# A mixture of softmaxes on one core: rows regrouped so that each partition holds 32 adjacent ones, weights on GpSimd, first batch loaded by head

## The chip, the cores and the metric

The kernel runs on one core of one Trainium2 chip. The metric is the device time in microseconds of that core. Before the change nine runs gave a median of 784.88 us (784.59 to 785.77).

## The reference

For each of 32 x 128 rows there are four heads of 4096 logits and four prior logits. The output row is the sum over the heads of the softmax of the head's logits, weighted by the softmax of the row's prior.

```python
batch, seq, vocab = 32, 128, 4096      # num_heads = 4, all float32
prior_probs = exp(prior - prior.max(-1));  prior_probs /= prior_probs.sum(-1)
softmax = exp(logits - logits.max(-1));    softmax /= softmax.sum(-1)
mixture = np.sum(prior_probs[..., None] * softmax, axis=2)
```

The logits are 268 MB, the output 67 MB, the prior 64 KB. Both kernels leave out the subtraction of the logits' maximum.

## The kernel before

One step of the outer loop (L85) handles one batch: 128 rows, one per partition, each with its four heads, so one tile `ltile` of 128 x 4 x 4096 (64 KB per partition, 8 MB). The sequence position is the partition, so the 128 rows of a tile are adjacent in memory, 64 KB apart, and the tile is one contiguous piece of 8 MB. The stored tile (128 x 4096, 2 MB) is contiguous too.

Loading: `load` (L41 to L46) is issued on SP's queue, as one transfer for batches 0 to 28 and as four transfers of one head each for the last three (`pieces`, L36). There are two `ltile` buffers, so the load of batch b+2 (L121) is issued when ACT has read all heads of batch b. Loads 0 and 1 are issued at the start (L53, L58).

The prior (L56 to L80) is loaded on ACT's queue with the batch on the partition (32 x 512), normalized on DVE and ACT, and turned into `pp` (sequence position on the partition) by 16 transposes of 32 x 32 blocks (L78).

Work on a head h: ACT takes the exponential of the head into `etile` (two buffers) and the row's sum into `dsum` (L100). DVE takes the reciprocal `rden` of the sum (L103), multiplies it by the prior's weight into `coeff` (L104), and then for head 0 writes `acc = etile * coeff` (L106, one tensor input), for heads 1 to 3 `acc = etile * coeff + acc` (L108, two tensor inputs). The small statistics come from a rotating pool of eight buffers. In the last two batches the exponential and the accumulation go into `ltile` itself (`inplace`).

Storing: batch b-1 is stored on ACT's queue during batch b (L90), for b below 29. Batches 28, 29, 30 and 31 are stored on SP's queue (L119 to L126), the last in two halves after each second of four chunks of the last accumulation (L112 to L119). There are two `acc` buffers, so L106 of batch b waits for the store of batch b-2.

The order on each engine is fixed when the kernel is built, by a scheduler that follows the program's order and its own estimates. In the kernel before, ACT has the first exponential of a batch ahead of the store of the batch before it from batch 3 on, and the store ahead in batches 1 and 2.

Of the kernel before, what the change touches and what calls it, by code (L numbers as in the profile page):

```python
# [1 line left out]

# [4 lines left out]

FP32 = mybir.dt.float32
AF = mybir.ActivationFunctionType
ALU = mybir.AluOpType  # L10
AX = mybir.AxisListType


@with_exitstack
def kernel(
    ctx: ExitStack,
    tc: tile.TileContext,
    logits: bass.AP,
    prior: bass.AP,
    out: bass.AP,  # L20
):
    nc = tc.nc
    B, S, H, V = logits.shape
    assert prior.shape == (B, S, H)
    assert out.shape == (B, S, V)
    P = 128
    assert S == P and B == 32

    lpool = ctx.enter_context(tc.tile_pool(name="lpool", bufs=2))
    epool = ctx.enter_context(tc.tile_pool(name="epool", bufs=2))  # L30
    apool = ctx.enter_context(tc.tile_pool(name="apool", bufs=2))
    spool = ctx.enter_context(tc.tile_pool(name="spool", bufs=8))
    cpool = ctx.enter_context(tc.tile_pool(name="cpool", bufs=1))


    def pieces(b):  # L36
        return 1 if b >= B - 3 else H

    ltiles = {}

    def load(b):  # L41
        lt = lpool.tile([P, H, V], FP32, name="ltile")
        n = pieces(b)
        for h in range(0, H, n):
            nc.sync.dma_start(out=lt[:, h : h + n], in_=logits[b, :, h : h + n, :])  # L45
        ltiles[b] = lt  # L46

    accs = {}

    def store(b, lo=0, hi=V, eng=nc.sync):  # L50
        eng.dma_start(out=out[b, :, lo:hi], in_=accs[b][:, lo:hi])  # L51

    load(0)  # L53


    pr = cpool.tile([B, S, H], FP32, name="pr")  # L56
    nc.scalar.dma_start(out=pr, in_=prior)
    load(1)  # L58
    pmax = cpool.tile([B, S], FP32, name="pmax")
    nc.vector.reduce_max(pmax, pr, axis=AX.X)  # L60
    pc = cpool.tile([B, S, H], FP32, name="pc")
    nc.vector.tensor_sub(pc, pr, pmax.unsqueeze(2).to_broadcast([B, S, H]))  # L62
    pe = cpool.tile([B, S, H], FP32, name="pe")
    nc.scalar.activation(pe, pc, AF.Exp)  # L64
    psum = cpool.tile([B, S], FP32, name="psum")
    nc.vector.reduce_sum(psum, pe, axis=AX.X)  # L66
    prec = cpool.tile([B, S], FP32, name="prec")
    nc.vector.reciprocal(prec, psum)  # L68

    pn = cpool.tile([B, H, S], FP32, name="pn")  # L70
    nc.vector.tensor_mul(  # L71
        pn.rearrange("b h s -> b s h"), pe, prec.unsqueeze(2).to_broadcast([B, S, H])
    )

    pp = cpool.tile([P, H, B], FP32, name="pp")
    for t in range(S // 32):
        for h in range(H):
            nc.vector.transpose(  # L78
                pp[32 * t : 32 * (t + 1), h, :], pn[:, h, 32 * t : 32 * (t + 1)]
            )  # L80

    NCHUNK = 4
    CW = V // NCHUNK

    for b in range(B):  # L85
        last = b == B - 1
        inplace = b >= B - 2
        lt = ltiles.pop(b)
        if 0 < b < B - 3:
            store(b - 1, eng=nc.scalar)  # L90
        if not inplace:
            accs[b] = apool.tile([P, V], FP32, name="acc")
        else:
            accs[b] = lt[:, 0]
        acc = accs[b]
        for h in range(H):
            split = last and h == H - 1
            et = lt[:, h] if inplace else epool.tile([P, V], FP32, name="etile")
            dsum = spool.tile([P, 1], FP32, name="dsum")
            nc.scalar.activation(et, lt[:, h], AF.Exp, accum_out=dsum)  # L100
            coeff = spool.tile([P, 1], FP32, name="coeff")
            rden = spool.tile([P, 1], FP32, name="rden")
            nc.vector.reciprocal(rden, dsum)  # L103
            nc.vector.tensor_mul(coeff, rden, pp[:, h, b : b + 1])  # L104
            if h == 0:
                nc.vector.tensor_scalar_mul(out=acc, in0=et, scalar1=coeff)  # L106
            elif not split:
                nc.vector.scalar_tensor_tensor(  # L108
                    out=acc, in0=et, scalar=coeff, in1=acc, op0=ALU.mult, op1=ALU.add
                )  # L110
            else:
                for c in range(NCHUNK):  # L112
                    cs = slice(c * CW, (c + 1) * CW)
                    nc.vector.scalar_tensor_tensor(  # L114
                        out=acc[:, cs], in0=et[:, cs], scalar=coeff, in1=acc[:, cs],
                        op0=ALU.mult, op1=ALU.add,
                    )
                    if c % 2:
                        store(b, (c - 1) * CW, (c + 1) * CW)  # L119
        if b + 2 < B:  # L120
            load(b + 2)  # L121
        if b == B - 3:
            store(b - 1)
            store(b)
        elif b == B - 2:
            store(b)  # L126


# [1 line left out]
_INS = ['logits', 'prior']  # L130
_OUTS = [((32, 128, 4096), 'float32')]


# [23 lines left out]
```

The softmax here doesn't subtract the row's maximum and nothing guards it: scores larger than these inputs give would overflow.

## Time and profile before

| what | value |
|---|---|
| median of 9 runs | 784.88 us |
| profiled execution, device time | 784.97 us |
| its span, first to last instruction | 783.2 us |
| DVE busy | 544.8 us, 408 instructions |
| ACT busy | 472.7 us, 258 instructions |
| POOL busy | 0.2 us, 4 instructions |
| exponential of a head (L100) | 3612 ns |
| first head's multiply (L106) | 2353 ns |
| multiply and add (L108) | 4484 ns |
| reciprocal, weight (L103, L104), one column | 158 and 159 ns |
| transfers: 8 MB load, 2 MB store on ACT's queue, issue to landing | 31.3 and 30.0 us |

DVE is the vector engine, ACT the scalar engine, POOL GpSimd, SP the engine whose queue issues the loads. The DMA line of the slices is the mean busy share of the core's 16 DMA engines, in tenths. Queue q1 is SP's, q10 is ACT's. A transfer of 128 rows is cut into packets of one row each: 64 KB for a whole row of logits, 16 KB for one head or one output row. The windows list gives busy time in us and, last, the DMA share and the bytes moved per time. A line of the waits gives who waited for whom, and then the total in us, the number of times and the longest.

### The profile page before, as it was taken

Reading aid. Unit: us, or ns where it says so; the run is one execution under the profiler, and the core shown is the slowest. Engines: PE = TensorE matmul, PEld = TensorE weight load, DVE = VectorE, ACT = ScalarE, POOL = GpSimd, SP = SyncE. Lnnn points to the kernel's source line nnn. Section 1 sums busy time; section 2 is a strip of 40 time slices with the busy share of each in tenths; the row PEclk is TensorE's granted clock in tenths of the full one; section 3 lists DMA queues with packets and bytes.
Section 4 is the critical chain, followed back from the end, with each engine's and each line's share of the span. In section 5 each row is a group of like instructions: output and inputs, shape, how many; then the busy total and the mean of one; then the engine's idle time right before and its main releaser. Section 6 shows DMA issues by size and latency. Waiting matters only on the chain.

```text
span 783.2 us, 977 instructions
## 1 busy us (share of the span) xinstructions
DVE 544.8 (70%) x408; ACT 472.7 (60%) x258; POOL 0.2 (0%) x4
## 2 busy tenths in 40 slices
DVE  3577688666786667866668766687656876669994
ACT  0766556755557555575555765556755567558971
POOL 0000000000000000000000000000000000000000
DMA  9999999999999999999999999999999999999997
GB/s 378 455 395 459 409 449 421 445 422 442 442 414 443 440 430 438 438 423 438 426 445 420 449 412 455 414 448 421 445 420 447 432 428 433 443 411 431 430 428 325
DMA packets 10712, 335.68 MB, mean 429 GB/s; under 512 B 1200, under 2 KB 1200, under 8 KB 1232
## 3 DMA queue, kind: packets, MB, share of 16 engines
q1 hardware_dynamic: 6624, 276.83, 81.9%
q10 hardware_dynamic: 4080, 58.79, 17.5%
q14 instruction: 8, 0.07, 0.0%
HBM read 268.50 MB, written 67.11 MB: 429 GB/s over the span
## 4 chain that ended last, share of the span: by engine, by line
DMA 76%; DVE 14%; ACT 6%; issue 1%; DVEq 0%; SPq 0%; ACTq 0%
DMA ltile<-in_logits_dram 42%; DMA out_dram<-acc 34%; DVE acc L108 9%; ACT etile L100 6%; DVE acc L106 3%; DVE ltile L108 1%; DVE ltile L114 0%; DVE coeff L104 0%; DVE rden L103 0%; DVE ltile L106 0%; DVEq L152 0%; SPq L45 0%; ACTq L100 0%; ACTq L51 0%; DVEq L106 0%
## 5 line engine op out<-in xcount | busy, mean ns | idle before, releaser
L100 ACT ACTIVATE etile<-ltile 128x4096 f32<-128x4096 f32 x120 | 433.4, 3612 | 277.3 <-DMA ltile<-in_logits_dram 199.2
L108 DVE SCALAR_TENSOR_TENSOR acc<-etile,coeff,acc 128x4096 f32<-128x4096 f32 x90 | 403.6, 4484 | 3.2
L103 DVE RECIPROCAL rden<-dsum 128x1 f32<-128x1 f32 x128 | 20.2, 158 | 157.8 <-ACT etile L100 157.8
L106 DVE TENSOR_SCALAR acc<-etile,coeff 128x4096 f32<-128x4096 f32 x30 | 70.6, 2353 | 49.6 <-DMA out_dram<-acc 49.4
L100 ACT ACTIVATE ltile<-ltile 128x4096 f32<-128x4096 f32 x8 | 28.9, 3611 | 4.8 <-DVE rden L103 2.4
L104 DVE TENSOR_TENSOR coeff<-rden,pp 128x1 f32<-128x1 f32 x128 | 20.3, 159 | 4.4
L108 DVE SCALAR_TENSOR_TENSOR ltile<-ltile,coeff 128x4096 f32<-128x4096 f32 x5 | 22.4, 4484 | 0.2
L100 ACT ACTIVATION_READ_ACCUMULATOR etile<-ltile 128x1 f32 x120 | 22.3, 186 | 0.0
L60 DVE TENSOR_REDUCE pmax<-pr 32x128 f32<-32x512 f32 x1 | 0.7, 674 | 10.9 <-DMA pr<-in_prior_dram 10.9
L64 ACT ACTIVATE pe<-pc 32x512 f32<-32x512 f32 x1 | 0.6, 628 | 9.9 <-DVE pc L62 9.9
L114 DVE SCALAR_TENSOR_TENSOR ltile<-ltile,coeff 128x1024 f32<-128x1024 f32 x4 | 4.9, 1278 | 0.0
L106 DVE TENSOR_SCALAR ltile<-ltile,coeff 128x4096 f32<-128x4096 f32 x2 | 4.7, 2354 | 0.1
L64 ACT ACT_TABLE_LOAD x1 | 1.3, 1283 | 1.2 <-PEq L141 1.2
L78 DVE STREAM_TRANSPOSE pp<-pn 32x32 f32<-32x32 f32 x16 | 1.9, 170 | 0.1
L100 ACT ACTIVATION_READ_ACCUMULATOR ltile<-ltile 128x1 f32 x8 | 1.5, 187 | 0.0
L66 DVE TENSOR_REDUCE psum<-pe 32x128 f32<-32x512 f32 x1 | 0.7, 674 | 0.7 <-ACT pe L64 0.7
L71 DVE TENSOR_TENSOR pn<-pe,prec 32x512 f32<-32x512 f32 x1 | 1.0, 1021 | 0.0
L68 DVE RECIPROCAL prec<-psum 32x128 f32<-32x128 f32 x1 | 0.9, 941 | 0.0
L62 DVE TENSOR_TENSOR pc<-pr,pmax 32x512 f32<-32x512 f32 x1 | 0.7, 678 | 0.0
L141 POOL MEMSET const-uint8-127<- 128x1 uint8 x1 | 0.1, 102 | 0.0
L141 POOL MEMSET const-bfloat16-1.0<- 128x1 bf16 x1 | 0.1, 101 | 0.0
L141 POOL MEMSET const-float32-0.0<- 128x1 f32 x1 | 0.1, 98 | 0.2 <-issue 0.2
(1 smaller groups left out, 0.1 us busy)
## 6 DMA issues: line engine op xcount, KB each, us to landing
out_dram<-acc ACTq DMA_DIRECT2D x28, 2048.0 KB, 30.0
ltile<-in_logits_dram SPq DMA_DIRECT2D x12, 2048.0 KB, 22.9
out_dram<-acc SPq DMA_DIRECT2D x2, 2048.0 KB, 34.1
out_dram<-ltile SPq DMA_DIRECT2D x1, 2048.0 KB, 22.8
out_dram<-ltile SPq DMA_DIRECT2D x2, 1024.0 KB, 10.2
ltile<-in_logits_dram SPq DMA_DIRECT2D x29, 31.3
pr<-in_prior_dram ACTq DMA_DIRECT2D x1, 64.0 KB, 10.2
```

The source lines that it names most:

```text
L60: nc.vector.reduce_max(pmax, pr, axis=AX.X)
L62: nc.vector.tensor_sub(pc, pr, pmax.unsqueeze(2).to_broadcast([B, S, H]))
L64: nc.scalar.activation(pe, pc, AF.Exp)
L68: nc.vector.reciprocal(prec, psum)
L71: nc.vector.tensor_mul(pn.rearrange("b h s -> b s h"), pe, prec.unsqueeze(2).to_broadcast([B, S, H]))
L78: nc.vector.transpose(pp[32 * t : 32 * (t + 1), h, :], pn[:, h, 32 * t : 32 * (t + 1)])
L100: nc.scalar.activation(et, lt[:, h], AF.Exp, accum_out=dsum)
L103: nc.vector.reciprocal(rden, dsum)
L104: nc.vector.tensor_mul(coeff, rden, pp[:, h, b : b + 1])
L106: nc.vector.tensor_scalar_mul(out=acc, in0=et, scalar1=coeff)
L108: nc.vector.scalar_tensor_tensor(out=acc, in0=et, scalar=coeff, in1=acc, op0=ALU.mult, op1=ALU.add)
L114: nc.vector.scalar_tensor_tensor(out=acc[:, cs], in0=et[:, cs], scalar=coeff, in1=acc[:, cs], op0=ALU.mult, op1=ALU.add,)
```

## The change

The rows are numbered 0 to 4095 (batch times sequence). In the new kernel partition p holds rows 32p to 32p+31, and step u of the outer loop handles row 32p+u of every partition. A tile therefore consists of 128 rows that lie 32 rows apart: 2 MiB from partition to partition in the logits, 512 KiB in the output. The prior is loaded with the same row assignment (128 x 32 x 4, 512 bytes per partition), is normalized in place and needs no transposes.

The other edits: step 0 is loaded by head, as the last three are. The statistics `dsum`, `rden` and `coeff` are one column each per head and step in fixed tiles of 128 columns. The two exponential buffers become one fixed tile `ebuf`, and the wait of an exponential for the exponential two before it is declared unneeded. Head 0 is multiplied by the reciprocal and by the weight in one DVE instruction with two scalars. For heads 1 to 3 GpSimd multiplies the weight, 96 instructions in all. The last accumulation is in two chunks rather than four, each stored at once. The first exponential of a step is kept in program order, so that on ACT it follows the store of the step before. On DVE the reciprocal of a head stands directly ahead of the large instruction of the same head.

```diff
+    U = B * S // P
+    lg = logits.rearrange("b s h v -> (b s) h v").rearrange("(p u) h v -> u p h v", u=U)
+    ov = out.rearrange("b s v -> (b s) v").rearrange("(p u) v -> u p v", u=U)
+    pv = prior.rearrange("b s h -> (b s) h").rearrange("(p u) h -> p u h", u=U)
...
     def pieces(b):
-        return 1 if b >= B - 3 else H
+        return 1 if b == 0 or b >= U - 3 else H
...
-            nc.sync.dma_start(out=lt[:, h : h + n], in_=logits[b, :, h : h + n, :])
+            eng.dma_start(out=lt[:, h : h + n], in_=lg[b, :, h : h + n, :])
...
-        eng.dma_start(out=out[b, :, lo:hi], in_=accs[b][:, lo:hi])
+        eng.dma_start(out=ov[b, :, lo:hi], in_=accs[b][:, lo:hi])
...
+    pr = cpool.tile([P, U, H], FP32, name="pr")
+    nc.scalar.dma_start(out=pr, in_=pv)
...
-    for t in range(S // 32):
-        for h in range(H):
-            nc.vector.transpose(
-                pp[32 * t : 32 * (t + 1), h, :], pn[:, h, 32 * t : 32 * (t + 1)]
-            )
...
-    NCHUNK = 4
+    NCHUNK = 2
...
+    dsum = cpool.tile([P, U * H], FP32, name="dsum")
+    rden = cpool.tile([P, U * H], FP32, name="rden")
+    coeff = cpool.tile([P, U * H], FP32, name="coeff")
+    ebuf = cpool.tile([P, 2, V], FP32, name="ebuf")
...
-            nc.scalar.activation(et, lt[:, h], AF.Exp, accum_out=dsum)
...
-            nc.vector.tensor_mul(coeff, rden, pp[:, h, b : b + 1])
+            i = b * H + h
+            col = slice(i, i + 1)
+            et = lt[:, h] if inplace else ebuf[:, h % 2]
+            ex = nc.scalar.activation(et, lt[:, h], AF.Exp, accum_out=dsum[:, col])
             if h == 0:
-                nc.vector.tensor_scalar_mul(out=acc, in0=et, scalar1=coeff)
+                tc.keep_in_program_order(ex)
+            if not inplace:
+                if len(exps) >= 2:
+                    tc.declare_no_dep(ex.ins, exps[-2], reason="covered by the sum")
+                exps.append(ex.ins)
+            nc.vector.reciprocal(rden[:, col], dsum[:, col])
+            if h == 0:
+                nc.vector.tensor_scalar(
+                    out=acc, in0=et, scalar1=rden[:, col], scalar2=pp[:, b, h : h + 1],
+                    op0=ALU.mult, op1=ALU.mult,
+                )
+                continue
+            nc.gpsimd.tensor_mul(coeff[:, col], rden[:, col], pp[:, b, h : h + 1])
```

More of the change, by code (lines that the diff above doesn't have):

```diff
@@ L27, with load @@
     assert S == P and B == 32
+    U = B * S // P
+    lg = logits.rearrange("b s h v -> (b s) h v").rearrange("(p u) h v -> u p h v", u=U)
+    ov = out.rearrange("b s v -> (b s) v").rearrange("(p u) v -> u p v", u=U)
+    pv = prior.rearrange("b s h -> (b s) h").rearrange("(p u) h -> p u h", u=U)
     lpool = ctx.enter_context(tc.tile_pool(name="lpool", bufs=2))
-    epool = ctx.enter_context(tc.tile_pool(name="epool", bufs=2))
     apool = ctx.enter_context(tc.tile_pool(name="apool", bufs=2))
-    spool = ctx.enter_context(tc.tile_pool(name="spool", bufs=8))
     cpool = ctx.enter_context(tc.tile_pool(name="cpool", bufs=1))
     def pieces(b):
-        return 1 if b >= B - 3 else H
+        return 1 if b == 0 or b >= U - 3 else H
     ltiles = {}
-    def load(b):
+    def load(b, eng=nc.sync):
         lt = lpool.tile([P, H, V], FP32, name="ltile")
@@ L50, in store @@
     def store(b, lo=0, hi=V, eng=nc.sync):
-        eng.dma_start(out=out[b, :, lo:hi], in_=accs[b][:, lo:hi])
[L53 to L59, printed above, removed]
-    nc.vector.reduce_max(pmax, pr, axis=AX.X)
[L61 to L72, printed above, removed]
-    )
-    pp = cpool.tile([P, H, B], FP32, name="pp")
-    for t in range(S // 32):
-        for h in range(H):
-            nc.vector.transpose(
-                pp[32 * t : 32 * (t + 1), h, :], pn[:, h, 32 * t : 32 * (t + 1)]
-            )
-    NCHUNK = 4
[L83 to L87, printed above, removed]
+        eng.dma_start(out=ov[b, :, lo:hi], in_=accs[b][:, lo:hi])
+    load(0, eng=nc.sync)
+    pr = cpool.tile([P, U, H], FP32, name="pr")
+    nc.scalar.dma_start(out=pr, in_=pv)
+    load(1, eng=nc.sync)
+    pmax = cpool.tile([P, U], FP32, name="pmax")
+    nc.vector.reduce_max(pmax, pr, axis=AX.X)
+    nc.vector.tensor_sub(pr, pr, pmax.unsqueeze(2).to_broadcast([P, U, H]))
+    nc.scalar.activation(pr, pr, AF.Exp)
+    nc.vector.reduce_sum(pmax, pr, axis=AX.X)
+    nc.vector.reciprocal(pmax, pmax)
+    pp = cpool.tile([P, U, H], FP32, name="pp")
+    nc.vector.tensor_mul(pp, pr, pmax.unsqueeze(2).to_broadcast([P, U, H]))
+    NCHUNK = 2
[3 more added lines that the diff above has]
+    ebuf = cpool.tile([P, 2, V], FP32, name="ebuf")
+    exps = []
+    for b in range(U):
+        last = b == U - 1
+        inplace = b >= U - 2
         lt = ltiles.pop(b)
-        if 0 < b < B - 3:
-            store(b - 1, eng=nc.scalar)
         if not inplace:
@@ L95 @@
         acc = accs[b]
+        if 0 < b < U - 3:
+            store(b - 1, eng=nc.scalar)
         for h in range(H):
             split = last and h == H - 1
[L98 to L103, printed above, removed]
@@ L104 @@
-            nc.vector.tensor_mul(coeff, rden, pp[:, h, b : b + 1])
-            if h == 0:
-                nc.vector.tensor_scalar_mul(out=acc, in0=et, scalar1=coeff)
-            elif not split:
+            i = b * H + h
+            col = slice(i, i + 1)
+            et = lt[:, h] if inplace else ebuf[:, h % 2]
+            ex = nc.scalar.activation(et, lt[:, h], AF.Exp, accum_out=dsum[:, col])
+            if h == 0:
+                tc.keep_in_program_order(ex)
[3 more added lines that the diff above has]
+                exps.append(ex.ins)
@@ new lines @@
+            nc.vector.reciprocal(rden[:, col], dsum[:, col])
[6 more added lines that the diff above has]
+            nc.gpsimd.tensor_mul(coeff[:, col], rden[:, col], pp[:, b, h : h + 1])
+            n = NCHUNK if split else 1
+            w = V // n
+            for c in range(n):
+                cs = slice(c * w, (c + 1) * w)
@@ L108 @@
                 nc.vector.scalar_tensor_tensor(
-                    out=acc, in0=et, scalar=coeff, in1=acc, op0=ALU.mult, op1=ALU.add
-                )
[L111 to L119, printed above, removed]
@@ L120 @@
-        if b + 2 < B:
+                    out=acc[:, cs], in0=et[:, cs], scalar=coeff[:, col], in1=acc[:, cs],
+                    op0=ALU.mult, op1=ALU.add,
+                )
+                if split:
+                    store(b, c * w, (c + 1) * w)
+        if b + 2 < U:
             load(b + 2)
-        if b == B - 3:
+        if b == U - 3:
             store(b - 1)
             store(b)
-        elif b == B - 2:
+        elif b == U - 2:
             store(b)
```

## The prediction

> **What bounds the kernel now.** I read the page's engine and slice parts first, then its queues, then the windows at both ends, then the waits and the timeline of the last batches.
>
> ```profile
> DVE 544.8 (70%) x408; ACT 472.7 (60%) x258; POOL 0.2 (0%) x4
> ...
> DMA  9999999999999999999999999999999999999997
> ...
> q1 hardware_dynamic: 6624, 276.83, 81.9%
> q10 hardware_dynamic: 4080, 58.79, 17.5%
> ...
> HBM read 268.50 MB, written 67.11 MB: 429 GB/s over the span
> ```
>
> No compute engine is full, but the 16 DMA engines are full in all slices but the last. In the queue lines the last column is the share of 16 engines over the span: q1 (SP) takes 81.9% of 783.2 = 641.4 us, q10 (ACT) 17.5% = 137.1 us, together 778.5 us. What is left, 4.7 us, is all the time in which the transfers do not fill the engines. q1 carries the loads (268.44 MB) and five late stores (8.39 MB); at 641.4/276.83 = 2.317 us per MB the loads cost 622.0 us. All stores, 67.11 MB at about 2.32, cost 155.9 us. A whole load row (64 KB, one packet) holds its engine for 64 KB/(434 GB/s/16) = about 2.42 us, a 16 KB row 0.61 us.
>
> ```profile
> 0.00:20.00 20.00, 5.91 (x21) 1.91 (x2) 0.20 (x4) 1.00 1.00 416
> ...
> 40.00:45.00 5.00, 4.72 (x4) 0.00 (x0) 0.00 (x0) 1.00 0.99 393
> 45.00:50.00 5.00, 0.90 (x3) 4.71 (x3) 0.00 (x0) 1.00 0.83 321
> ...
> 160.00:400.00 240.00, 165.61 (x118) 147.27 (x80) 0.00 (x0) 1.00 1.00 432
> ...
> 765.00:770.00 5.00, 4.93 (x6) 0.81 (x2) 0.00 (x0) 1.00 1.00 429
> 770.00:775.00 5.00, 1.92 (x2) 0.00 (x0) 0.00 (x0) 1.00 0.97 413
> 775.00:784.00 9.00, 0.00 (x0) 0.00 (x0) 0.00 (x0) 1.00 0.41 172
> ```
>
> Columns: window, length, DVE, ACT and POOL busy, clock, DMA share, GB/s. There is one hole near 45 us (0.83) and the drain after 775 us (172 GB/s x 9 us = 1.55 MB, 3.6 us of work, so some 5 us of landing and closing). In the middle there is no hole.
>
> ```profile
> ACT etile L100 <- DMA ltile<-in_logits_dram: 199.2, 27, 10.0
> DVE rden L103 <- ACT etile L100: 157.8, 33, 9.0
> ACT etile L100 <- DVE rden L103: 60.7, 54, 1.5
> DVE acc L106 <- DMA out_dram<-acc: 49.4, 26, 2.3
> ```
>
> These waits confirm it: ACT waits for loads 27 times, DVE then waits for ACT. A batch needs 2.35 + 3 x 4.48 + 4 x 0.35 = 17.2 us of DVE against (622.0 + 155.9)/32 = 24.3 us of DMA, so DVE has 7 us of cover per batch. The cover is absent at the end only: in the timeline DVE works without a pause from 719 to 772 us.
>
> **What the Trainium skill says.** (1) "DMA: Bandwidth & Descriptors", Latency and other measured facts: copies of tiles of 128 partitions x 16 KiB between HBM tensors reach 214 GB/s per direction at full rate, 207 with a row pitch of 512 KiB, 164 with 2 MiB, 103 with 4 or 8 MiB; that channels alias is called an inference there. The trace of before has no such pitch: its partitions are 64 KB apart in the loads and 16 KB apart in the stores, and it moves 429 GB/s in both directions together, which agrees with 2 x 214 as the full rate. (2) The same page, Where 436 GB/s comes from: 435 GB/s is the ceiling of the ports. The trace's 432 in mid-run agrees, so no layout can make transfers appreciably faster. (3) "VectorE: DVE Perf Modes", The perf-mode tier table: fp32 tensor_scalar from SBUF runs at two elements per cycle (1227 ns for 2048). L106 with 2353 ns for 4096 agrees. (4) "GPSIMD Engine Reference", 3.1: a two-input elementwise op costs about 2.6 cycles per element after dispatch, 4497 ns for 2048. No run here shows it on one column.
>
> **The change, part by part.**
>
> *32 adjacent rows per partition.* Same bytes and packet lengths, but partition p now starts at row 32p: in HBM neighbouring partitions of a load are 32 x 64 KB = 2 MiB apart, those of a store 32 x 16 KB = 512 KiB. These are exactly two pitches of the skill's table. As an estimate from that page: loads take 214/164 = 1.305 times as long, 622.0 x 1.305 = 811.7 us, +189.7; stores 214/207 = 1.034 times, 155.9 x 1.034 = 161.2, +5.3. Nothing covers this, since DMA sets the end. The price is uncertain on three sides. Its rows are 16 KiB, ours 64 KB in 28 of 32 batches; if longer rows do not alias, nothing is added there (lower end 0). The page's figure is a pair of a load and a store; if all its loss is the load's, the load factor is 2 x 1.305 - 1 = 1.61 and the loads take 1001 us. If the memory limits reads to 2 x 164 = 328 GB/s while stores fill the remaining engine time, the loads' 268.44/0.328 = 818 us is the whole. I take equal factors, the middle.
>
> *Batch 0 by head.* Four 2 MB loads in place of one 8 MB; ACT starts at the first head, not at 23.00 us, and is done with batch 0 by about 10 + 4 x 3.8 = 25 us (the prior, whose chain precedes it on ACT, landed at 10.9) instead of 39. Load 2 waits for that on SP; it can then be queued behind load 1, which needs the engines until about 39. The hole closes: 0.17 x 5 at 45 us and the smaller shortfalls around it come to about 2 us, -2. The prior's 128 short packets replace 32, each alternating with 16 KB instead of 64 KB loads; a few us either way are covered by that same slack.
>
> *Weights on GpSimd.* 96 one-column multiplies leave DVE (L104, 159 ns + 30 ns of gap), replaced by DVE -> POOL -> DVE. In DVE's new order the reciprocal stays directly ahead of the big multiply that now waits for POOL, so DVE's later work and, two heads on, ACT's buffer queue behind the hand-over. Its bounds: 0.1 us (POOL's one-column MEMSETs take 98 to 102 ns) and 1.0 us, generously; I take 0.35. That is (0.35 - 0.19) x 3 = +0.5 us per batch, at most +2.4. DVE's 7 us per batch hide it in the middle. At the tail four batches (28 to 31) run with little cover, +2 us on DVE, at most +10, less what follows.
>
> *First head by two scalars.* Removes 32 multiplies, -0.19 us each. The large op stays one-source fp32, so 2353 ns (if it lost the double rate, 4.3 us: still covered in the middle). *Fixed columns, two chunks, dropped waits.* The 16 transposes (1.9 us) and the wider prior arithmetic lie ahead of the first logits; nothing. Four chunks of 1278 ns become two: a 4096-wide op takes 4484, so 209 + 1.044 ns per column, 2 x 2.35 against 5.11, -0.4 us at the end. The dropped ACT waits are on ACT itself; ACT's last releaser is the load or DVE, so nothing. The store now precedes the next batch's first exp on ACT: it waits for DVE, which is done about 2 us before that batch lands; this shortens L106's wait of up to 2.3 us, which DMA hides. SP's order is the same apart from three more issues at the start.
>
> *Sum.* 811.7 + 161.2 + 4.7 + 0.6 (small packets and rounding) - 2 = 976.2 us of span; with slower loads DVE's tail has more cover and adds nothing. The profiled execution took 784.97 against a span of 783.2, so 1.8 us lie around it; it stands 0.1 us from the median of 784.88. Forecast 978 us.
>
> **The rivals.**
> *Memory keeps up (not slower).* One mechanism: the engine's 2.42 us per row, not memory, stays the limit, since only about 347 GB/s of reads are asked for and a 64 KB row spreads wider than a 16 KB row. It decides if the mean row stays under about 2.43 us (2 us over 232 rows per engine). Then -2 from the head remains, with the tail's +2 - 0.4 - 0.8 (four first heads) partly in its place: 782.5 to 783.5, say 783; bounds 781 to 787. For it: every slice is engine-bound today. Against it: the table's 164 was measured below that same engine limit.
> *Only the short rows suffer.* The four batches loaded by head (128 rows of 16 KB per engine) pay 128 x 0.611 x 0.305 = 23.9 us, stores 5.3: 783 + 29 = 812.
> *Reads reach only 164 GB/s on their own,* as a limit per direction: 268.44/0.164 = 1637, about 1640 us. It speaks against it that the page's number may be set by reads and writes together.
> *GpSimd's hand-over becomes the bound:* with 1 us it costs 2.4 us per batch under a cover of 7, and at most 8 at the tail: 791, only if memory keeps up.
>
> **How the numbers follow.** Aliasing in all loads 0.64: from 826 (818 + 8 of ends) through 978 to 1162 (1001 + 156 + 5), with 0.07 of it beyond that, toward 1640. Short rows only 0.08. Memory keeps up 0.28: of it 0.17 are faster by over 0.2%, 0.07 within, 0.04 slower (the tail). Two tenths of a per cent, 1.6 us, is about what a measurement of this kernel can tell from no change. So faster 0.17, same 0.07, slower 0.76. The range goes from 781 to 1162; the likeliest case's own is 826 to 1162.
>
> **What would show it.** Right: q1's share of engine time per MB up by 1.3, full DMA slices at 330 to 350 GB/s in mid-run, load issue-to-landing well over 31 us, ACT's wait for loads doubled or more; stores' time per MB nearly as before; no hole near 45 us; L111 at 2.35 us. Wrong: mid-run still at 432 GB/s (then memory keeps up and the ends decide), slow rates only in the first 20 and last 60 us (short rows), or DVE waiting on POOL longer than 1 us.

## The result, and the profile after

The changed kernel took 803.28 us (median of ten runs, 801.31 to 811.25) against 784.84 for the kernel before beside it: a ratio of 1.0246 with a 95% interval of 1.023 to 1.0262, so 18.4 us slower where 193 us were forecast. The profiled execution took 801.31 us, its span 799.5 us, 16.3 us more than before; it was the fastest of the ten. One run of all that follow counts as slow and is left out of its median: 844.46 us of the changed kernel in a later series, over 3% above the fastest beside it.

The page of the changed kernel, the lines that answer to those shown of before (busy time of the engines, DMA share in 40 slices, the queues, the traffic):

```profile
DVE 524.3 (66%) x262; ACT 469.8 (59%) x258; POOL 18.4 (2%) x100
...
DMA  8999999999999999999999999999999999999997
...
q1 hardware_dynamic: 7056, 276.83, 82.2%
q10 hardware_dynamic: 4176, 58.79, 17.2%
...
HBM read 268.50 MB, written 67.11 MB: 420 GB/s over the span
...
ltile<-in_logits_dram SPq DMA_DIRECT2D x28, 33.1
```

The bytes are the same, and the DMA engines are as full as before, yet they move 420 instead of 429 GB/s. The shares must be turned into time: q1 takes 82.2% of 799.5 = 657.2 us of the 16 engines, 15.8 us more than before; q10 takes 17.2% = 137.5 us, 0.4 more. (A share is rounded to 0.1%, 0.8 us.) What is left of the span is 4.8 us, as before. So nearly the whole difference lies in how long the packets of the load queue take. From issue to landing an 8 MB load takes 33.1 us (the last line) against 31.3 before and 32.3 with the other edits alone (e2_edits_only, below). Taking the five late stores on q1 off at 19.5 us, the loads went from 622.0 to 637.7 us, a factor of 1.025.

The windows of the changed kernel (same columns as before, DMA share and GB/s last):

```profile
0.00:20.00 20.00, 5.76 (x9) 9.11 (x7) 0.39 (x5) 1.00 0.88 352
...
40.00:45.00 5.00, 0.00 (x0) 0.00 (x0) 0.00 (x0) 1.00 0.88 354
45.00:50.00 5.00, 0.00 (x0) 0.19 (x1) 0.00 (x0) 1.00 1.14 472
...
160.00:400.00 240.00, 157.71 (x77) 141.09 (x78) 5.30 (x28) 1.00 1.00 428
...
785.00:790.00 5.00, 2.92 (x2) 0.00 (x0) 0.00 (x0) 1.00 0.98 418
790.00:800.00 10.00, 0.00 (x0) 0.00 (x0) 0.00 (x0) 1.00 0.49 209
```

In mid-run the engines are full at 428 GB/s against 432 before: the forecast's 330 to 350 is not there. ACT stands still from 28.4 us and DVE from 33.4 us; they wait for load 1, which landed at 49.81 us. The waits of the changed kernel:

```profile
ACT ebuf L100 <- DMA ltile<-in_logits_dram: 254.8, 31, 21.4
DVE rden L109 <- ACT ebuf L100: 222.1, 60, 20.2
ACT ebuf L100 <- DVE acc L121: 43.4, 31, 1.4
DVE acc L121 <- POOL coeff L116: 27.3, 90, 0.3
...
DVE acc L111 <- DMA out_dram<-acc: 1.2, 4, 0.5
```

The two instructions that are new in form, from the page:

```profile
L111 DVE TENSOR_SCALAR acc<-ebuf,rden,pp 128x4096 f32<-128x4096 f32 x30 | 72.4, 2413 | 2.2 <-DMA out_dram<-acc 1.2
L116 POOL TENSOR_TENSOR coeff<-rden,pp 128x1 f32<-128x1 f32 x96 | 18.2, 190 | 764.6 <-DVE rden L109 764.6
```

ACT's wait for loads grew from 199.2 to 254.8 us; as it is 241.8 us with the other edits alone (e2), most of this growth is not from slower loads. The hand-over to POOL costs DVE 27.3/90 = 0.30 us each time; L111's wait for the store is almost gone (49.4 to 1.2 us). Neither is seen in the time, because DMA sets the end.

The trace's records of the single packets tell how the loads slowed. The typical 64 KB packet did not change; a part of them got long (counted from the records of the two traces):

```
64 KB load packets        median   mean    more than 3% above 2418 ns
before                    2418 ns  2426 ns   2%
changed kernel            2418 ns  2477 ns  24%
16 KB store packets on ACT's queue: mean 611 ns in both
```

### The profile page after: what moved, and what is told of

Its sections match the earlier page's. It is cut to its first block, busy times and chain, and to the rows that moved or that the text cites. A ratio compares the mean times of both kernels' runs of the same rounds, so it can differ in the third digit from the quotient of the medians.

```text
span 799.5 us, 847 instructions
## 1 busy us (share of the span) xinstructions
DVE 524.3 (66%) x262; ACT 469.8 (59%) x258; POOL 18.4 (2%) x100
## 3 DMA queue, kind: packets, MB, share of 16 engines
q1 hardware_dynamic: 7056, 276.83, 82.2%
q10 hardware_dynamic: 4176, 58.79, 17.2%
## 4 chain that ended last, share of the span: by engine, by line
DMA 66%; ACT 15%; DVE 10%; issue 7%; POOL 0%; DVEq 0%; SPq 0%; POOLq 0%; ACTq 0%
DMA ltile<-in_logits_dram 66%; ACT ebuf L100 15%; DVE acc L121 10%; ACT ltile L100 0%; POOL coeff L116 0%; DVE rden L109 0%; DVE ltile L121 0%; DVEq L159 0%; SPq L49 0%; POOLq L159 0%; ACTq L100 0%
## 5 line engine op out<-in xcount | busy, mean ns | idle before, releaser
L100 ACT ACTIVATE ebuf<-ltile 128x4096 f32<-128x4096 f32 x120 | 433.0, 3609 | 298.2 <-DMA ltile<-in_logits_dram 254.8
L121 DVE SCALAR_TENSOR_TENSOR acc<-ebuf,coeff,acc 128x4096 f32<-128x4096 f32 x90 | 403.6, 4484 | 27.3 <-POOL coeff L116 27.3
L111 DVE TENSOR_SCALAR acc<-ebuf,rden,pp 128x4096 f32<-128x4096 f32 x30 | 72.4, 2413 | 2.2 <-DMA out_dram<-acc 1.2
L116 POOL TENSOR_TENSOR coeff<-rden,pp 128x1 f32<-128x1 f32 x96 | 18.2, 190 | 764.6 <-DVE rden L109 764.6
L121 DVE SCALAR_TENSOR_TENSOR ltile<-ltile,coeff 128x4096 f32<-128x4096 f32 (+1 forms) x7 | 27.0, 3874 | 1.8 <-POOL coeff L116 1.8
L100 ACT ACTIVATION_READ_ACCUMULATOR ebuf<-ltile 128x1 f32 x120 | 22.4, 186 | 0.0
L111 DVE TENSOR_SCALAR ltile<-ltile,rden,pp 128x4096 f32<-128x4096 f32 x2 | 4.8, 2412 | 0.1
## 6 DMA issues: line engine op xcount, KB each, us to landing
ltile<-in_logits_dram SPq DMA_DIRECT2D x28, 33.1
```

Of the source, the lines that this page charges most:

```text
L100: ex = nc.scalar.activation(et, lt[:, h], AF.Exp, accum_out=dsum[:, col])
L111: nc.vector.tensor_scalar(out=acc, in0=et, scalar1=rden[:, col], scalar2=pp[:, b, h : h + 1], op0=ALU.mult, op1=ALU.mult,)
L116: nc.gpsimd.tensor_mul(coeff[:, col], rden[:, col], pp[:, b, h : h + 1])
L121: nc.vector.scalar_tensor_tensor(out=acc[:, cs], in0=et[:, cs], scalar=coeff[:, col], in1=acc[:, cs], op0=ALU.mult, op1=ALU.add,)
```

## The experiments

Theory: the power-of-two distance between the partitions of a load makes load packets collide in memory, but by far less than the forecast took. (That they collide is the theory; what the traces show is that they take longer.) First rival: placement costs nothing, the other edits do. Second rival: it is not the power of two but the wide scatter over memory.

### Each half of the change alone

```diff
 # e1_rows_only, on the kernel before (the layout of the prior follows the rows, not shown)
-            nc.sync.dma_start(out=lt[:, h : h + n], in_=logits[b, :, h : h + n, :])
+            nc.sync.dma_start(out=lt[:, h : h + n], in_=lg[b, :, h : h + n, :])
...
-        eng.dma_start(out=out[b, :, lo:hi], in_=accs[b][:, lo:hi])
+        eng.dma_start(out=ov[b, :, lo:hi], in_=accs[b][:, lo:hi])
...
 # e2_edits_only, on the changed kernel (prior and transposes as before, not shown)
-    lg = logits.rearrange("b s h v -> (b s) h v").rearrange("(p u) h v -> u p h v", u=U)
-    ov = out.rearrange("b s v -> (b s) v").rearrange("(p u) v -> u p v", u=U)
+    lg = logits
+    ov = out
...
```

> The kernel before with the regrouped rows alone (and the prior in the matching layout, without transposes). Theory 1, the placement of the rows in HBM makes the load packets longer: about 802 us, with SP's queue at about 657 us of engine time instead of 641. Theory 2, the regrouping costs nothing and the other edits (by-head start, hand-over to GpSimd, order on ACT) do: 783 to 786 us.

> The changed kernel with the rows of the kernel before (batch by batch, prior transposed as before), all other edits kept. Theory 1: 782 to 784 us, and the packets as short as before. Theory 2: about 800 us.

The rows alone took 822.54 us (ratio 1.0481, 1.0459 to 1.0503), the other edits alone 783.95 us (0.9988, 0.9981 to 0.9994). The placement is the cause; the first rival falls. The packet records agree: a 64 KB packet took 2545 ns on average with the rows alone and 2422 ns with the edits alone. But 822.5 is more than the whole change cost, and more than the expected 802. That needed more runs (below). The edits alone are the fastest version of all, 0.12% below the kernel before. In them ACT already waits long for loads:

```profile
ACT ebuf L113 <- DMA ltile<-in_logits_dram: 241.8, 32, 18.2
...
ltile<-in_logits_dram SPq DMA_DIRECT2D x28, 32.3
```

The queue line and the windows of the rows alone show how long the loads took and where the long packets lie:

```profile
q1 hardware_dynamic: 6624, 276.83, 82.5%
...
0.00:20.00 20.00, 0.00 (x0) 1.28 (x1) 0.20 (x4) 1.00 0.94 320
20.00:40.00 20.00, 7.02 (x11) 10.44 (x6) 0.00 (x0) 1.00 1.01 368
40.00:60.00 20.00, 14.65 (x13) 12.34 (x9) 0.00 (x0) 1.00 0.97 382
60.00:160.00 100.00, 66.86 (x46) 57.39 (x31) 0.00 (x0) 1.00 1.00 417
160.00:400.00 240.00, 166.63 (x118) 139.50 (x78) 0.00 (x0) 1.00 1.00 423
```

82.5% of 820.3 us, less the stores, is 657.2 us of loads, a factor of 1.057. The engines are nearly full in every row, and the rate climbs from 320 to 423 GB/s although every step reads at the same distances. In its first 20 us the kernel before moves 416 GB/s at a share of 1.00; at the share of 0.94 here 320 stands for 340, so the packets of the start take 416/340 = 1.22 times as long. That comes near the forecast's factor, but it doesn't stay.

### The distance: 31, 32, 16 and 8 rows

```diff
 # e3_pitch31, on the changed kernel
-    lg = logits.rearrange("b s h v -> (b s) h v").rearrange("(p u) h v -> u p h v", u=U)
+    lg = logits.rearrange("b s h v -> (b s) h v")
...
-            eng.dma_start(out=lt[:, h : h + n], in_=lg[b, :, h : h + n, :])
+            eng.dma_start(out=lt[:, h : h + n], in_=lg[b : b + 31 * (P - 1) + 1 : 31, h : h + n, :])
...
 # e8_adj8, on the changed kernel (e9_adj16: 16 for 8 throughout)
-    lg = logits.rearrange("b s h v -> (b s) h v").rearrange("(p u) h v -> u p h v", u=U)
+    lg = logits.rearrange("b s h v -> (b s) h v").rearrange("(g p u) h v -> g u p h v", p=P, u=8)
...
-            eng.dma_start(out=lt[:, h : h + n], in_=lg[b, :, h : h + n, :])
+            eng.dma_start(out=lt[:, h : h + n], in_=lg[b // 8, b % 8, :, h : h + n, :])
```

> The changed kernel with loads whose partitions lie 31 rows (1.94 MiB) apart instead of 32 (2 MiB): the same number of bytes and packets, but it reads row 31p+u where 32p+u is meant, so some rows are read twice and others never. Theory 1a, the power of two of the distance is what costs: 782 to 785 us. Theory 1b, any wide scatter over HBM costs (pages, distance): about 802 us, as the changed kernel.

> The changed kernel with loads whose partitions hold 8 adjacent rows, so 512 KiB from partition to partition instead of 2 MiB (the rows then don't match the prior and the output). If the loss grows with the power of two, as the skill's table has it: 784 to 788 us. If any power of two costs alike: about 802 us.

> The same with 16 adjacent rows, 1 MiB from partition to partition. If the loss grows with the distance: 788 to 797 us. If only 2 MiB and above cost: 784 us. If any power of two costs alike: about 802 us.

At 31 rows, 1.94 MiB, the loss is gone: 784.64 us, ratio 0.9994 (0.9986 to 1.0002). Its queue lines:

```profile
q1 hardware_dynamic: 7056, 276.83, 82.0%
q10 hardware_dynamic: 4176, 58.79, 17.5%
```

82.0% of its span of 783.2 us is 642.2 us, as before the change (641.4), with the same packets, nearly the same scatter (260 of the 268 MB) and the same other edits; the mean 64 KB packet is back at 2423 ns. So the exact distance decides, and the second rival falls. At 512 KiB the time was 786.16 us (1.002, 1.0013 to 1.0028), at 1 MiB 810.16 us (1.0328, 1.0299 to 1.0356); the 2 MiB kernel beside these two took 815.17. The 1 MiB run thus missed its 788 to 797: the loss doesn't grow evenly with the distance, most of it is there at 1 MiB. A step also spans less memory there (64 and 128 MB), but e3 shows that a wide span alone costs nothing. All this fits large powers of two; 31 rows is the only distance tried that is not a power of two.

The packet records add what the times hide: at 1 MiB the mean 64 KB packet took 2535 ns, more than the 2510 ns of the 2 MiB kernel beside it, while the 16 KB packets of the same queue took 620 ns against 665 (617 at 31 rows).

### Short packets

All steps by head, so all load packets are 16 KB, at 2 MiB (e4) and in the old rows at 64 KB (e5, on the other edits alone):

```diff
-        return 1 if b == 0 or b >= U - 3 else H
+        return 1
```

> The changed kernel with every step loaded by head, so that all load packets are 16 KB at a distance of 2 MiB, the condition of the skill's table. If the table's factor of 1.305 belongs to short rows: about 960 to 990 us. If short rows lose no more per byte than long ones: 800 to 812 us.

> Every step loaded by head, with the other edits, but in the rows of the kernel before (64 KB between partitions): the control for the regrouped by-head run of 870.7 us. If the loss there is the 2 MiB distance: 784 to 788 us. If it is the short packets or the many transfers: 850 us or more.

870.68 us (1.1093, 1.1072 to 1.1114) against 790.32 us (1.0067, 1.0053 to 1.0081). So loading by head costs some 6 us in the old rows too (783.95 without it, in another series), a little more than the 784 to 788 expected; the rest of e4's loss belongs to the distance. The queue lines of e4, then q1 of e5:

```profile
q1 hardware_dynamic: 19152, 276.83, 83.1%
q10 hardware_dynamic: 4176, 58.79, 15.7%
...
q1 hardware_dynamic: 19152, 276.83, 82.5%
```

83.1% of its span of 875.4 us is 727.5 us; less 19.5 us of stores that is 708.0 us of loads, a factor of 1.138 to the 622.0 of before. (The profiled execution was the slowest of five; at the median it would be some 1.128.) e5 ends at (82.5% of 788.5 - 19.5)/622.0 = 1.014. Against long rows in the same series (e1, 0.057) short rows lose a little over twice as much, yet not 0.305. The changed kernel's 0.025 comes from another series, and series differ, as shown below. Both numbers of the expectation for e4 were missed; the truth lies between. Nor is the order of long and short fixed: at 1 MiB the long packets lost and the short ones hardly did (above).

### What makes the start so slow, and what is the share of the series

The first 60 us suggested that the engines begin in step and drift apart, and that the by-head start breaks the step. Three runs were to show it. The first two differ from the changed kernel and from the rows alone by one condition each:

```diff
 # e10_no_head0, on the changed kernel
-        return 1 if b == 0 or b >= U - 3 else H
+        return 1 if b >= U - 3 else H
...
 # e11_rows_head0, on the rows alone
-        return 1 if b >= B - 3 else H
+        return 1 if b == 0 or b >= B - 3 else H
...
 # e13_no_stores, on the rows alone
-        if 0 < b < B - 3:
-            store(b - 1, eng=nc.scalar)
...
         if b == B - 3:
-            store(b - 1)
             store(b)
```

> The changed kernel with step 0 loaded in one transfer of 64 KB packets, all else kept. Theory A, the engines alias while they march in step, and the by-head start breaks the step: the first 60 us at a load factor of 1.2 to 1.3 as with the rows alone, 811 to 816 us. Theory B, the by-head start is not what separates the changed kernel from the rows alone: 802 to 805 us.

> The regrouped rows with the by-head start and no other edit. Theory A: 808 to 814 us, the first 60 us as in the changed kernel. Theory B: 820 to 825 us; if it reaches 802 us, the start alone explains the whole difference of 19 us.

> The regrouped rows alone, with the stores of steps 0 to 28 left out (only the last three outputs are written): loads only, in long packets at 2 MiB distance. If the early factor of 1.3 is due to the absence of stores (all engines loading), it stays near 1.3 throughout: 622 x 1.3 + 20 = about 830 us. If it is due to the engines starting in step and drifting apart, it fades within 100 us: about 660 us; without any aliasing 268.4 MB at 432 GB/s would be 622 us plus 13 us of late stores and ends.

Without the by-head start the changed kernel took 799.32 us, the rows with it 800.73. Set beside the earlier 803.28 and 822.54 the two contradict each other: removing the start costs nothing, adding it seems to save 22 us. Neither theory A (the by-head start breaks the step) nor B (it doesn't matter) holds both. Without stores the kernel took 685.01 us, neither 830 nor 660. Its queue line and windows:

```profile
q1 hardware_dynamic: 6480, 274.73, 97.7%
...
0.00:20.00 20.00, 0.00 (x0) 1.28 (x1) 0.20 (x4) 1.00 0.96 340
20.00:40.00 20.00, 8.81 (x11) 11.11 (x7) 0.00 (x0) 1.00 1.00 398
40.00:60.00 20.00, 16.61 (x13) 14.62 (x8) 0.00 (x0) 1.00 0.99 390
60.00:160.00 100.00, 81.04 (x61) 70.34 (x39) 0.00 (x0) 1.00 1.00 405
160.00:400.00 240.00, 199.59 (x139) 169.42 (x93) 0.00 (x0) 1.00 0.99 410
```

The slow start fades with loads alone too, so it is not the lack of stores that makes it; but it settles at 410, not at 432 GB/s. 97.7% of 685.0 us less 14.6 us for the 6.29 MB of late stores is 654.6 us of loads, a factor of 1.052: loads alone lose about as much as loads with stores beside them. Why the start is the slowest stretch stays open: a drift of the engines was not tried apart from the addresses, which move on with every step.

The contradiction left one suspect: the series. Runs of one series share a chip and stand beside each other; e1 and e10/e11 did not. So the same kernels were run again, unaltered, side by side:

> The changed kernel unaltered, beside the rows alone on one chip. If the earlier gap of 19 us between the two belongs to the kernels: 801 to 805 us here, and the rows alone at 820 to 825. If it belongs to the chip or to where the arrays lie: the two within 5 us of each other.

> The rows alone unaltered, same chip as the run before. Kernel's own: 820 to 825 us. Chip's or the placement's: within 5 us of the changed kernel.

> The changed kernel, one of four on one chip. If the by-head start protects: this and the rows with by-head start near each other and at least 8 us below the two without. If the call decides: all four within 6 us of each other. If the other edits protect: the changed kernel with and without by-head start together, both below the rows with and without it.

> The rows alone, one of the four: by-head start protects, 8 us or more above the rows with by-head start; call decides, within 6 us of all.

> The changed kernel without by-head start, one of the four: by-head start protects, 8 us or more above the changed kernel; call decides, within 6 us of all.

> The rows with by-head start, one of the four: by-head start protects, near the changed kernel; call decides, within 6 us of all.

| series | changed kernel | without by-head start | rows alone | rows with by-head start | kernel before |
|---|---|---|---|---|---|
| result | 803.28 | | | | 784.84 |
| with e1 to e4 | | | 822.54 | | 784.84 |
| with e10, e11 | | 799.32 | | 800.73 | 784.93 |
| with e14, e15 | 815.17 | | 822.75 | | 784.79 |
| e16 to e19 | 818.72 | 817.60 | 818.87 | 820.78 | 784.90 |

e14 and e15 lie 7.6 us apart, which is neither of their two cases. In the last series, the only one with all four, the four lie within 3.2 us, the case that the expectations name "call decides". The changed kernel itself moves from 803.28 to 818.72 between series (1.0246 to 1.0432 of the kernel before) while the kernel before stays within 0.2 us. Neither the by-head start nor the other edits protect from the loss by an amount that repeats, and the theory of the protecting start is given up. The 19 us between e1 and the result are put down to the series; the changed kernel was not run beside e1 itself. The four series of the experiments in this table ran on four chips (8, 4, 2 and 10 in order; the result's is not recorded), so whether the chip or the place of the arrays in its memory makes the difference can't be told.

### Two terms of the sum

```diff
 # e7_stores_regrouped, on the changed kernel
-    lg = logits.rearrange("b s h v -> (b s) h v").rearrange("(p u) h v -> u p h v", u=U)
+    lg = logits
...
 # e20_edits_no_head0, on the other edits alone
-        return 1 if b == 0 or b >= U - 3 else H
+        return 1 if b >= U - 3 else H
```

> The changed kernel with contiguous loads, batch by batch, and regrouped stores alone, 512 KiB from partition to partition (rows and prior then don't match). If the forecast's store factor of 1.034 holds: 789 us. If stores lose nothing at that distance: 783.5 to 784.5 us, as the other edits alone (783.95).

> The other edits in the old rows, without the by-head start. If that start closes a hole worth 2 us: 786 us, against 783.95 with it. If the hole closes by itself or something else takes its place: 783.5 to 784.5 us.

Regrouped stores with contiguous loads: 785.05 us, ratio 1.0002 (0.9994 to 1.0011), half a microsecond above the case of no loss. Its queue line:

```profile
q10 hardware_dynamic: 4176, 58.79, 17.5%
```

17.5% of 783.3 = 137.1 us, as before: the stores' own packets lose nothing at 512 KiB. The other edits without by-head start: 784.00 us (0.9989, 0.9981 to 0.9997), against 783.95 with it in another series: the start gains nothing. It does move a wait, at no cost in time: with the start (e2, first line) DVE's first multiply of a step hardly waits, without it (e20) it waits 57.5 us in all for stores:

```profile
L124 DVE TENSOR_SCALAR acc<-ebuf,rden,pp 128x4096 f32<-128x4096 f32 x30 | 72.4, 2412 | 1.1
...
L124 DVE TENSOR_SCALAR acc<-ebuf,rden,pp 128x4096 f32<-128x4096 f32 x30 | 72.4, 2413 | 57.6 <-DMA out_dram<-acc 57.5
```

## Why the prediction was wrong

**The direction and the place were right.** It named the regrouping as the one costly edit, in the time of SP's load packets, with the DMA slices still full. e2 and e3 show it: at 64 KB and at 1.94 MiB between the partitions nothing is lost.

**The step that failed** is "As an estimate from that page: loads take 214/164 = 1.305 times as long, 622.0 x 1.305 = 811.7 us, +189.7". The term measured 622.0 to 637.7 us, factor 1.025, +15.7 (in a series with a larger loss 1.057, the rows alone of e1). Two things were wrong with it. It took a figure for 16 KiB rows, as the step itself noted, and set it on 64 KB rows at full value: in one series 16 KB rows lost 0.138 (e4) and long rows 0.057 (e1). And even 16 KB rows reached 1.138 only. The measurement in the Trainium skill ("DMA: Bandwidth & Descriptors", Latency and other measured facts) copies between two memory tensors laid out at the same distance, so reads and writes both have it; here one fifth of the bytes are stores at 512 KiB. Loads without those stores lost as much (e13, 1.052), so the stores don't soften the loss; stores at 2 MiB were not tried. Why 1.305 is not reached stays open. The prediction had a rival with long rows spared ("Only the short rows suffer", 812 us); its time came near the measured one, but by the wrong account, so the nearness is luck: the packet records put 13.3 of the changed kernel's 17.2 us of lengthening on the 64 KB packets, and only 4.0 on the 16 KB ones.

**The point of "Memory keeps up".** A mean row below 2.43 us was to decide; it came out at 2.477 us, just above. The half-way case, a small fraction of packets colliding, had no number of its own in the cases, though the range reached over it. Of the signs set for a loss, the load's landing (33.1 against 31.3 us) and ACT's wait (254.8 against 199.2) moved the right way, but far less than written, and much of both came from the other edits (32.3 and 241.8 us in e2). (The 232 long rows per engine in that case are those of the kernel before; the changed kernel has 224.)

**Stores, +5.3.** Nothing: e7, 137.1 us on q10.

**By-head start, -2.** Nothing: e20 against e2. The hole near 45 us was read from a window whose neighbour gives all of it back, 10 x 0.09 against 5 x 0.17:

```profile
50.00:60.00 10.00, 9.01 (x7) 8.60 (x5) 0.00 (x0) 1.00 1.09 469
```

A share above 1 says that the windows don't book packets exactly, and the 4.7 us of unfilled time were all there was to gain from.

**Weights on GpSimd.** Taken as 0.35 us a time, measured 0.30 (POOL's instruction lasts 190 ns); hidden, as said: e2 has all 96 and is not slower. The tail held less cover than foreseen for slower loads: in the last batch DVE waited for the exponential only 0.16 and 0.28 us.

**First head by two scalars.** The double rate was kept: 2413 ns against 2353, so 60 ns more and not 4.3 us. **Chunks, transposes, waits, order of stores** cost nothing; but the earlier store did not shorten the wait for stores: e20 has it and waits 57.5 us, against 49.4 before. It is the by-head start that takes the wait away (e2), and the time did not move for it. All these edits together gain 0.9 us (e2).

## What to carry to other kernels

In a kernel that fills its DMA engines, the addresses of a transfer are part of its price: look at the time per MB of each queue, not at whether the engines are busy, because an engine with lengthened packets looks just as busy (82.2% of the span here, 81.9% before). Keep the partitions of a load off large powers of two (1.94 instead of 2 MiB cost nothing here), but don't carry a loss factor from one row length to another: in one series it was 1.057 for most rows at 64 KB and 1.138 at 16 KB. And repeat a run beside its rival before reading a difference of two per cent between series, above all for a kernel whose time depends on where its data lies.

## What the runs showed of the hardware that was not expected

- Loads at 2 MiB between partitions start at 320 to 340 GB/s and climb to 410 to 423 within some 160 us, at unchanged distances, with stores and without (e1, e13). Why was not shown.
- In the changed kernel the loss is a tail: the median 64 KB packet keeps its 2418 ns, while 24% of them are more than 3% longer (2% before).
- Loads lose at 1 MiB nearly what they lose at 2 MiB (810.16 and 815.17 us in one series), and little at 512 KiB (786.16); at 1 MiB the long packets carry it (2535 ns against 620 ns for 16 KB). Stores at 512 KiB lose nothing (611 ns per packet).
- The loss varies from series to series, for the changed kernel from 2.5% to 4.3%, while the medians of the contiguous kernel repeat within 0.2 us.
- A one-column multiply on POOL takes 190 ns and leaves the waiting DVE idle for 0.30 us, the hand-over there and back included.
